# Planner durations, buffers for row sums, early weight loads and a folded softmax scale in an attention stage

## The chip, the cores and the metric

The kernel runs on one core of one Trainium2 chip. The metric is the device time of one execution in microseconds (us). Five engines take part: TensorE (PE, with its weight loads as PEld), VectorE (DVE), ScalarE (ACT), GpSimd (POOL) and SyncE (SP), which here only starts transfers. Each engine works through its own queue in the order of the program and meets the others at semaphores.

## The reference

The program is a decoder trunk of two layers over 1040 positions (16 learned ones ahead of 1024) and width 1024, in float32. Layer 0 mixes tokens with a recurrent scan and a pooling mixer; layer 1, which the change concerns, with differential attention of 8 heads, each with two sets (c = 0, 1) of 64-wide queries and keys and one set of 128-wide values:

```
def one_block(args):                       # a block of 128 queries
    qblk, start = args
    s = jnp.einsum('bqhcd,bkhcd->bhcqk', qblk, k).astype(jnp.float32) * scale   # scale = 64 ** -0.5 = 1/8
    qpos = start + jnp.arange(Q_BLOCK)
    mask = kpos[None, :] <= qpos[:, None]
    s = jnp.where(mask, s, -jnp.inf)
    p = jax.nn.softmax(s, axis=-1)
    attn = p[:, :, 0] - lam * p[:, :, 1]
    return jnp.einsum('bhqk,bkhe->bqhe', attn.astype(v.dtype), v)

o = rmsnorm(causal_diff_attention(q, k, v, lam), subln_w, SUBLN_EPS) * (1.0 - lam_init)
m = o.reshape(B, L, D_MODEL) @ w_out
h = h + rmsnorm(m, g[1])
f = sq_relu_mlp(rmsnorm(h, g[2]), mlp_w1[i], mlp_w2[i])
h = h + rmsnorm(f, g[3])
```

The 16 learned positions are dropped from the output; their queries are not computed in layer 1.

## The kernel before, in words

`Trunk.run` calls four stages: `mixer0`, `late(0)`, `mixer1`, `late(1)`. A mixer ends with its output projection begun, and `late` finishes the projection and does both norms and the MLP. Full float32 products are made of three passes of a rounded format: each operand is split into a high part (a cast on ScalarE, for instance `opb<-raw`) and a low part (a subtraction on VectorE or POOL), and `mm3` multiplies high by high, low by high and high by low.

The order of `mixer1` isn't the order of its code. A `Recorder` stands in for the five engines: `Recorder.call` notes each instruction with the tiles that it reads and writes and with a planned duration (`cost`), and `Flow.order` then lists them anew, each engine always taking, of what could start first, the task with the longest way to the end. The list is then issued as it stands (all these instructions carry line 298 in the profile, the replay in `call`), and each engine's queue has that order. So a planned duration changes no instruction, but the places of instructions on all engines. `late` has a `Flow` of its own, with its own durations (`F.act`, `F.dve`, `F.pe`), which are not touched.

`mixer1`, per head: `attn_in` projects queries, keys and values of the next head in three stretches of columns (`rows`, `vals`; PSUM tiles of the two-buffer ring `dps`), turns queries and keys by position (`ab`), regroups them through transfers (`qkd<-ab`, in `heads`) and splits them (`halves`: `qst` for the queries, `kh` and `kl` for the keys, the latter on VectorE and POOL). `turn` transposes and splits the values (tiles that are called `spare` too). `attn_block` does the softmax of one block of 128 queries for both c, over 144, 272, ... 1040 keys: score matmuls into `s` (ring `sps`, two buffers of 1024 columns; the last 16 of 1040 in a tile `tr` of the one-buffer ring `tps`), row maxima in `m` (the tile `m2`), exponentials on ScalarE into `vt` and `p` (the tiles p0 and p1; `vt` is the name of the buffer that p0 shares) with row sums to `m`, a reciprocal, and the difference of both. `attn` transposes the weights (`tr`), splits them (`ah`) and multiplies with the values (`av`, ring `aps`, one buffer). The head's output goes to DRAM (`o1d<-cau`) and is loaded back (`ho<-o1d`) as an operand `opa` of the output projection. `early` computes the first part of that projection beside head 7, and writes it with `part<-pz`.

Row sums for the input norm: `settle` multiplies a stretch of accumulated squares (`rsa`) by ones on TensorE into a tile of `psum()`, which is the ring `dps`, and takes the reciprocal root. `mixer1` calls it for stretches 1 and 2.

In `late(1)` the rest of the projection needs five raw weight tiles: two of `in_wl` (640 columns used), then three of `in_wo`. Each is loaded (line 677), cast (678) and subtracted (679) into the operands `opb`; the stored first part returns with `ac<-part` (681), and line 699 multiplies into `bank`. For layer 0 the first two raw tiles are loaded in `mixer0`.

Of the kernel before, what the change touches and what calls it, by code (L numbers as in the profile page):

```python
# [7 lines left out]
F32 = mybir.dt.float32  # L8
F32R = mybir.dt.float32r
AF = mybir.ActivationFunctionType  # L10
ALU = mybir.AluOpType
# [3 lines left out]
P = 128  # L15
T = 1040
NM = 16
# [46 lines left out]
LW = ((768, 768, 1024, 1024), (640, 640, 1024, 1024, 1024))  # L64
# [138 lines left out]
class Recorder:  # L203
# [60 lines left out]
    def call(self, eng, op, args, kw):  # L264
        aps = [x for x in list(args) + list(kw.values()) if hasattr(x, "tensor") and hasattr(x, "ap")]
        out = kw.get("out", args[0] if args else None)
        w = [out] + ([kw["accum_out"]] if kw.get("accum_out") is not None else [])
        r = [x for x in aps if not any(x is y for y in w)]
        n = max(math.prod(int(k) for k in x.shape[1:]) for x in aps)
        psum = any(x.space == PSUM for x in aps)  # L270
        size = 0
        if op.startswith("dma"):
            cost = {"POOL": 1.0, "SP": .47}.get(eng, .38)
            words = math.prod(int(k) for k in out.shape)
            run = min(self.run_of(x) for x in aps)
            size = words / run * (8 + .0367 * 4 * run) / 16e3 * 350e3
        elif eng == "PE":
            cols, x = math.prod(int(k) for k in args[0].shape[1:]), args[1]
            if op == "transpose":
                cost = .115  # L280
            elif x.dtype == F32R:
                cost = max(cols / 2400 + .014, .108)
            elif x.dtype == F32:
                cost = 2 * max(2 * cols / 2400 + .003, .111)
            else:
                cost = max(cols / 2400 + .01, .06)
        elif eng == "DVE":
            column = any(x.shape[-1] == 1 for x in aps)
            cost = n / (480 if op == "tensor_tensor_scan" else 960) + .07 + (.06 if column else 0.0) + (.08 if psum and out.shape[0] < P else 0.0)
        elif eng == "ACT":  # L290
            wide = max(len(x.shape) for x in aps) > 2
            cost = n / (1200 if wide or not psum else 1700) + (.165 if wide and psum else .2 if wide else .1)
            cost += sum(.09 for k in ("scale", "bias") if hasattr(kw.get(k), "ap"))
        else:
            cost = n / 450 + .15
        fn = getattr(getattr(self.real, {"PE": "tensor", "DVE": "vector", "ACT": "scalar", "POOL": "gpsimd", "SP": "sync"}[eng]), op)
        port = eng == "POOL" or eng == "DVE" and not psum and len(aps) > 2
        one = eng, cost, lambda: fn(*args, **kw), r, w  # L298
        if self.held is not None:
            self.held.append(one)  # L300
        else:
            self.keep(eng, cost, [one[2]], r, w, port and not size, size)
# [27 lines left out]
class Trunk:  # L330
# [156 lines left out]
    def rows(self, d, t0, W):  # L487
        return d.rearrange("(k p) t -> p k t", p=P)[:, :, t0:t0 + W]

    def settle(self, t0, W):  # L490
        acc = self.rsa[:, t0:t0 + W]
        ps = self.psum()[:, :W]
        self.nc.tensor.matmul(ps, self.con[:, K_ONE:K_ONE + P], acc, start=True, stop=True)
        self.rsqrt(ps, 1024, 1e-6, acc, self.tmp("rp", 3)[:, :W])

# [66 lines left out]
    def late(self, l, xs, part, hin, hmid, hout, pre, rsb):  # L562

        nc, tc, A = self.nc, self.tc, self.A
# [32 lines left out]
        S = [rp.tile([P, NH], F32, name=f"ss{i}") for i in (0, 1)]  # L597
# [71 lines left out]
        n = self.lw_n  # L669
        rl = [[("L", i, 0), ("L", i, 1)] + [c for b, a in self.lw_at[i] for c in nX(("B", b), 0, 4 * NH)] for i in range(len(n))]  # L670
        for i in range(len(n)):
            hi, lo = self.lw(i)
            if True:
                z = ("R", i % 4 // 2, i % 2)
                raw = R[i % 4 // 2][:, i % 2, :n[i]]
                if l or i > 1:
                    F.dma(lambda raw=raw, i=i: nc.sync.dma_start(raw, self.lw_src(l, i)), n[i] * 512, w=[z])
                F.act(n[i], lambda raw=raw, hi=hi: nc.scalar.copy(hi, raw), r=[z], w=[("L", i, 0)])  # L678
                F.dve(n[i], lambda raw=raw, hi=hi, lo=lo: tt(lo, raw, hi.bitcast(F32), op=ALU.subtract), r=[z, ("L", i, 0)], w=[("L", i, 1)])
            if i < 2:  # L680
                F.dma(lambda h=i: nc.sync.dma_start(m[h][:, :ne], self.rows(part, off + NH * h, NH)), ne * P * 4 * NH, w=sum((nM(i, k) for k in range(ne)), []))
# [209 lines left out]
        n, hs = H  # L891
# [753 lines left out]
    def mixer1(self, hn):  # L1645
# [4 lines left out]
        with tc.tile_pool(name="dps", bufs=2, space=PSUM, reuse_waits="tile") as dps, \  # L1650
# [47 lines left out]
            for h in range(8):  # L1698
# [5 lines left out]
                i = 0  # L1704
# [10 lines left out]
            for c in range(4):  # L1715
                xs[c].append(self.x7[c])
            self.late_x = xs
            rec.flow.run()
        self.nc = tc.nc
        return part  # L1720

    def attn_in(self, h, hn):
# [7 lines left out]
        def rows(nme, c):  # L1730
            q = nme == "q"
            t0, W = CH[c]
            if c == 0:
                if h:
                    w[nme] = self.weights(self.A["w_qkv"][(0 if q else 8) + h])
                tl[nme] = ep.tile([P, T], F32, tag="ab", name=self.nm("ab"), bufs=2)
            off = NM if (q and c == 0) else 0
            if h == 0 and c < 2:
                ps = self.first[nme][:, c * 512:c * 512 + 512]
            else:  # L1740
                ps = self.dps.tile([P, 512], F32, tag="d", name=self.nm("psq"))
                project(nme, c, ps, off)
            if h == 0 and nme == "k":
                if c > 0:
                    self.settle(t0, W)
                for j in (0, 1):
                    z = cs[:, j, t0:t0 + W]
                    nc.vector.tensor_tensor(z, z, self.rsa[:, t0:t0 + W], op=ALU.mult)
            s = slice(t0 + off, t0 + W)
            ab = tl[nme]  # L1750
            b = ep.tile([P, CW], F32, tag="rp", name=self.nm("rp"), bufs=3)
            nc.vector.tensor_tensor(b[0:64, off:W], ps[64:128, off:W], cs[64:128, 1, s], op=ALU.mult)
            nc.vector.tensor_tensor(b[64:128, off:W], ps[0:64, off:W], cs[0:64, 1, s], op=ALU.mult)
            nc.vector.tensor_tensor(ab[:, s], ps[:, off:W], cs[:, 0, s], op=ALU.mult)
            nc.gpsimd.tensor_tensor(ab[:, s], ab[:, s], b[:, off:W], op=ALU.add)
# [15 lines left out]
        def halves(nme):  # L1771
            for c in (0, 1):
                d = tl[nme, c]
                if nme == "q":
                    st = ep.tile([P, 1024], F32R, tag="qst", name=self.nm("qst"), bufs=2)
                    nc.scalar.copy(st, d[:, :1024])
                    nc.vector.tensor_tensor(st[64:128], d[64:128, :1024], st[64:128].bitcast(F32), op=ALU.subtract)
                    res["q", c] = st
                else:
                    kh = ep.tile([P, T], F32R, tag="kh", name=self.nm("kh"), bufs=2)  # L1780
                    kl = ep.tile([P, T], F32R, tag="kl", name=self.nm("kl"), bufs=2)
                    nc.scalar.copy(kh, d)
                    for a, b, e in ((0, 640, nc.vector), (640, T, nc.gpsimd)):
                        e.tensor_tensor(kl[:, a:b], d[:, a:b], kh[:, a:b].bitcast(F32), op=ALU.subtract)
                    res["k", c] = (kh, kl)
# [36 lines left out]
    def attn_block(self, h, i, qkv):  # L1822
# [7 lines left out]
        for c in (0, 1):  # L1830
# [18 lines left out]
                        nc.tensor.matmul(out(x0, x1), self.identb, self.maskb[:, x0 - m0:x1 - m0], start=False, stop=True)  # L1849
            S.append(sp)  # L1850
            if L > 512:
                nc.vector.tensor_reduce(m2[:, c:c + 1], sp[:, :L0], axis=mybir.AxisListType.X, op=ALU.max)
        if L <= 512:
            s3 = S[0].rearrange("p (c k) -> p c k", c=2)[:, :, :L]
            nc.vector.tensor_reduce(m2[:, 0:2], s3, axis=mybir.AxisListType.X, op=ALU.max)
        if se is not None:
            nc.vector.tensor_reduce(m2[:, 4:6], se[:, :2 * NM].rearrange("p (c k) -> p c k", c=2),
                                    axis=mybir.AxisListType.X, op=ALU.max)
            nc.vector.tensor_tensor(m2[:, 0:2], m2[:, 0:2], m2[:, 4:6], op=ALU.max)
        nc.vector.tensor_scalar(m2[:, 0:2], m2[:, 0:2], -0.125, None, op0=ALU.mult)  # L1860
        pr = []
        for c in (0, 1):
            p = ep.tile([P, T], F32, tag=f"p{c}", name=self.nm("p"), bufs=1 if c else 3)
            nc.scalar.activation(p[:, :L0], S[c][:, :L0], AF.Exp, bias=m2[:, c:c + 1], scale=0.125, accum_out=m2[:, 2 + c:3 + c])
            if se is not None:
                nc.scalar.activation(p[:, 1024:T], se[:, c * NM:(c + 1) * NM], AF.Exp, bias=m2[:, c:c + 1], scale=0.125,
                                     accum_out=m2[:, 6 + c:7 + c])
            pr.append(p)
        if se is not None:
# [238 lines left out]
```

## Time and profile before

| what | value |
|---|---|
| median of 3 runs | 2774.11 us (2773.92 to 2783.99) |
| profiled execution, its time | 2776.32 us |
| its span in the trace | 2774.5 us |
| its mean granted TensorE clock | 0.973 |
| attention stage in the trace, with the handover | about 1410 to 2037.5 us |
| of it a steady head | 66.0 us |

The profile is of one execution. A row of the timeline has its start and its length (of all instructions in the row where x2 or more stands at its end), the engine, the line, the operation, what it writes and reads, and, in brackets, how long the engine was idle before and which engine's work ended that. In the tables of stretches `PEclk` is the TensorE clock that was granted, as a share of full speed.

### The profile page before, as it was taken

The page shows a single profiled execution, that of the slowest core. Times are in us where ns is not written, and L with a number is a line of the kernel's source. Part 1 is how long each engine was busy: PE and PEld are TensorE (multiplying, and loading weights), DVE is VectorE, ACT ScalarE, POOL GpSimd, SP SyncE. Part 2 cuts the span into 40 slices and gives each one's busy share as a digit, 9 for nine tenths or more (in the row PEclk, how much of TensorE's full clock was granted, in tenths as well). Part 3 has the DMA queues.
Part 4 walks back from the last instruction along what each step waited for, and adds up shares of the span by engine and source line. Part 5 has one row for each costly group of instructions (what it writes and reads, how often), then busy time and mean ns, then how long its engine had stood idle before and what let it go on. Part 6 is the DMA issues. An engine that isn't in the chain of part 4 may idle for free.

```text
span 2774.5 us, 44830 instructions
## 1 busy us (share of the span) xinstructions
PE 2613.0 (94%) x16950; PEld 2378.8 (86%) x16950; DVE 2021.7 (73%) x3742; ACT 1344.0 (48%) x2779; POOL 289.9 (10%) x410
## 2 busy tenths in 40 slices
PE   7999998899999999999969999998989999999997
PEld 6899897899899999999967888887887788778877
DVE  5356867534977777888787777777538778778888
ACT  6456766544633334343345555555636333443343
POOL 0111334220000000000023222222000000000000
PEclk9999999899999999999989999998999999999998
DMA  4456777554324345443332222222143243543443
GB/s 155 168 184 190 239 218 221 179 161 151 143 102 169 137 163 194 168 154 135 109 120 74 65 69 62 62 60 83 55 147 144 106 167 136 193 187 137 152 159 122
DMA packets 198576, 391.28 MB, mean 141 GB/s; under 512 B 59984, under 2 KB 122328, under 8 KB 185944
## 3 DMA queue, kind: packets, MB, share of 16 engines
q1 hardware_dynamic: 171176, 348.24, 37.7%
q10 hardware_dynamic: 27184, 40.18, 4.0%
q8 instruction: 133, 2.18, 0.3%
q14 instruction: 83, 0.68, 0.1%
HBM read 240.06 MB, written 131.38 MB: 134 GB/s over the span
## 4 chain that ended last, share of the span: by engine, by line
PE 60%; DVE 11%; ACT 5%; issue 2%; DMA 2%; POOL 0%; SPq 0%; DVEq 0%; ACTq 0%; POOLq 0%
PE bank L699 43%; PE ps L298 9%; PE s L298 2%; PE av L298 2%; ACT vt L298 1%; PE tr L298 1%; DVE m L298 1%; PE xs L298 1%; ACT p L298 1%; DVE opb L826 1%; DVE ac L1080 1%; DMA hh<-hid 1%; DVE ac L1081 1%; DVE vt L298 1%; DVE ac L1009 1%
## 5 line engine op out<-in xcount | busy, mean ns | idle before, releaser
L699 PE MATMUL bank<-opa,wp 128*128 128x260 f32 (+1 forms) x3296 | 657.5, 319 | 8.3 <-DVE wp L790 4.9
L699 PEld LDWEIGHTS bank<-opa,wp 128*128 128x128 f32 x3296 | 516.9, 188 | 59.7 <-DVE wp L790 6.4
L298 PE MATMUL ps<-opa,wp 128*128 128x346 f32 (+3 forms) x1600 | 345.5, 326 | 7.9 <-DVE spare L298 2.7
L699 PE MATMUL bank<-opb,wp 128*128 128x260 f32 (+1 forms) x1150 | 347.5, 323 | 1.8 <-DVE ac L1009 1.8
L298 PEld LDWEIGHTS ps<-opa,wp 128*128 128x128 f32 x1600 | 260.7, 191 | 20.0 <-issue 4.7
L298 PE MATMUL ps<-opa,whi 128*128 128x346 f32 (+2 forms) x1008 | 269.1, 329 | 4.9 <-DVE ys L298 4.2
L699 PE MATMUL bank<-opa,hh 128*128 128x260 f32 (+1 forms) x1112 | 241.1, 321 | 7.9 <-DVE hh L790 5.3
L699 PEld LDWEIGHTS bank<-opb,wp 128*128 128x128 f32 x1150 | 216.2, 188 | 20.9 <-issue 2.2
L1009 DVE TENSOR_TENSOR ac<-bank,ac 128x520 f32<-128x520 f32 (+1 forms) x256 | 171.5, 691 | 67.5 <-PE bank L699 66.1
L699 PE MATMUL bank<-opa,opb 128*128 128x260 f32 (+4 forms) x1168 | 207.1, 307 | 13.4 <-ACT opb L678 10.1
L699 PEld LDWEIGHTS bank<-opa,hh 128*128 128x128 f32 x1112 | 185.8, 191 | 24.4 <-DVE hh L790 5.8
L699 PEld LDWEIGHTS bank<-opa,opb 128*128 128x128 f32 x1168 | 169.2, 195 | 24.3 <-ACT opb L678 10.5
L298 PEld LDWEIGHTS ps<-opa,whi 128*128 128x128 f32 x1008 | 181.7, 193 | 6.8 <-DVE ys L298 5.0
L699 PE MATMUL bank<-opb,hh 128*128 128x260 f32 (+1 forms) x616 | 180.4, 326 | 0.0
L789 ACT CAST wp<-raw 128x512 fp32r<-128x512 f32 (+1 forms) x138 | 80.4, 584 | 185.2 <-PE bank L699 181.2
L298 PE MATMUL ps<-opa,wlo 128*128 128x346 f32 (+2 forms) x504 | 158.6, 315 | 0.0
L789 ACT CAST wp<-ss 128x512 fp32r<-128x512 f32 (+1 forms) x130 | 76.7, 590 | 164.3 <-PE bank L699 143.5
L699 PE MATMUL bank<-opa,tt 128*128 128x260 f32 (+1 forms) x648 | 130.4, 318 | 0.2 <-DVE tt L790 0.2
L699 PEld LDWEIGHTS bank<-opb,hh 128*128 128x128 f32 x616 | 117.6, 191 | 10.0
L298 POOL TENSOR_TENSOR wpx<-raw,wp 128x1024 fp32r<-128x1024 f32 (+1 forms) x14 | 35.2, 2516 | 817.2 <-PE bank L699 742.5
L699 PE MATMUL bank<-opb,opb 128*128 128x256 f32 (+4 forms) x456 | 111.3, 307 | 0.5 <-DVE tt L755 0.5
L699 PEld LDWEIGHTS bank<-opa,tt 128*128 128x128 f32 x648 | 102.1, 188 | 9.5 <-DVE tt L790 0.4
(372 smaller groups left out, 5820.5 us busy)
## 6 DMA issues: line engine op xcount, KB each, us to landing
raw<-in_w_dram SPq DMA_DIRECT2D x64, 1024.0 KB
hid<-ac SPq DMA_DIRECT2D x14, 1820.0 KB
hid<-ac SPq DMA_DIRECT2D x14, 1792.0 KB
hh<-hid SPq DMA_DIRECT2D x23, 1040.0 KB
hh<-hid SPq DMA_DIRECT2D x23, 1024.0 KB
pk<-sg ACTq DMA_DIRECT2D x32, 704.0 KB
lt<-pk SPq DMA_DIRECT2D x32, 704.0 KB
raw<-in_w_qkv_dram SPq DMA_DIRECT2D x24, 512.0 KB
```

Source lines behind the costliest of these rows:

```text
L298: one = eng, cost, lambda: fn(*args, **kw), r, w
L699: nc.tensor.matmul(ps, use(x), use(y), start=start and i == j == 0, stop=i == len(ws) - 1 and j == 2, skip_group_check=not start)
L789: F.act(n, lambda: nc.scalar.copy(use(t[0][:, :n]), src), r=rd, w=[z[0]] + claim)
L826: F.dve(4 * NH, lambda: tt(lo, use(src), hi.bitcast(F32), op=ALU.subtract), r=rd + wh, w=wl)
L1009: F.dve(NH, lambda d=d, q=q: tt(sv(d), q, sv(d), op=ALU.add), r=nq + nd, w=nd, ps=True)
L1080: F.dve(W, lambda d=d, k=k: stt(d, d, self.gcol(l, 3, k), y, op0=ALU.mult, op1=ALU.mult), r=nd + [ny], w=nd)
L1081: F.dve(W, lambda d=d, k=k: tt(d, d, use(H3[k // 4][:, k % 4, :W]), op=ALU.add), r=nd + [("H", k // 4, k % 4)], w=nd)
```

## The change

Five edits, all in or around `mixer1`:

1. Planned durations in `Recorder.call`: a starting float32r matmul of 400 columns or more counts 0.085 us more; ScalarE's work on PSUM of 400 columns or more counts n/1200 + 0.06 in place of n/1700 + 0.1; an accumulated row sum (`accum_out`) 0.1 more.
2. `settle` takes its PSUM tile from the ring `tps` (stretch 1) and `aps` (stretch 2) in place of `dps`.
3. The loads of the two raw `in_wl` tiles of layer 1 are recorded at the end of `mixer1`, not in the flow of `late(1)`.
4. The queries are scaled by 1/8 where they are split: the cast becomes an `activation` with a scale, the subtraction a `scalar_tensor_tensor`. The exponentials lose their scale.
5. The row maxima are written negated (`negate=True`), the two parts of the longest block are joined with `min`, and the multiplication of `m` by -1/8 goes.

```diff
             elif x.dtype == F32R:
-                cost = max(cols / 2400 + .014, .108)
+                cost = max(cols / 2400 + .014, .108) + (.085 if cols >= 400 and kw.get("start") else 0.0)
...
             cost = n / (1200 if wide or not psum else 1700) + (.165 if wide and psum else .2 if wide else .1)
+            if psum and n >= 400:
+                cost = n / 1200 + .06
+            if kw.get("accum_out") is not None:
+                cost += .1
...
-    def settle(self, t0, W):
+    def settle(self, t0, W, pool, tag):
         acc = self.rsa[:, t0:t0 + W]
-        ps = self.psum()[:, :W]
+        ps = pool.tile([P, 512], F32, tag=tag, name=self.nm("ps"))[:, :W]
...
-                if l or i > 1:
+                if i > 1:
                     F.dma(lambda raw=raw, i=i: nc.sync.dma_start(raw, self.lw_src(l, i)), n[i] * 512, w=[z])
...
             self.late_x = xs
+            self.lw_n = LW[1]
+            for i in (0, 1):
+                nc.sync.dma_start(self.R[0][:, i, :self.lw_n[i]], self.lw_src(1, i))
             rec.flow.run()
...
-                    self.settle(t0, W)
+                    self.settle(t0, W, *((self.tps, "tr"), (self.aps, "av"))[c - 1])
...
-                    nc.scalar.copy(st, d[:, :1024])
-                    nc.vector.tensor_tensor(st[64:128], d[64:128, :1024], st[64:128].bitcast(F32), op=ALU.subtract)
+                    nc.scalar.activation(st, d[:, :1024], AF.Copy, scale=0.125)
+                    nc.vector.scalar_tensor_tensor(st[64:128], d[64:128, :1024], 0.125, st[64:128].bitcast(F32), op0=ALU.mult, op1=ALU.subtract)
...
-                nc.vector.tensor_reduce(m2[:, c:c + 1], sp[:, :L0], axis=mybir.AxisListType.X, op=ALU.max)
+                nc.vector.tensor_reduce(m2[:, c:c + 1], sp[:, :L0], axis=mybir.AxisListType.X, op=ALU.max, negate=True)
...
-            nc.vector.tensor_tensor(m2[:, 0:2], m2[:, 0:2], m2[:, 4:6], op=ALU.max)
-        nc.vector.tensor_scalar(m2[:, 0:2], m2[:, 0:2], -0.125, None, op0=ALU.mult)
+            nc.vector.tensor_tensor(m2[:, 0:2], m2[:, 0:2], m2[:, 4:6], op=ALU.min)
...
-            nc.scalar.activation(p[:, :L0], S[c][:, :L0], AF.Exp, bias=m2[:, c:c + 1], scale=0.125, accum_out=m2[:, 2 + c:3 + c])
+            nc.scalar.activation(p[:, :L0], S[c][:, :L0], AF.Exp, bias=m2[:, c:c + 1], accum_out=m2[:, 2 + c:3 + c])
```

The lines of the kernel after stand four lower (298 is 302 there), and a tile in a shared buffer goes by the name of the first that used it: the ring of `tr` begins with a `ps`, that of `av` with another `ps`, and the ring `dps` is called `psv`.

TensorE at the start of `mixer1`, where the products of the first values begin. Before, the row sum of stretch 1 stands there alone:

```order
L298 MATMUL s_1_13729<-opa_75,wp_6334 128x346
L298 MATMUL ps_0_13735<-rsa,con 128x346
L298 MATMUL ps_1_13736<-opa_70,spare_0_13737 128x348
L298 MATMUL ps_1_13736<-opa_70,spare_0_13739 128x348
L298 MATMUL ps_1_13736<-opa_70,spare_0_13737 128x348 x2
```

The one of stretch 2 stands some fifty rows on, among the products of a projection:

```order
L298 MATMUL ps_1_13736<-opa_76,wp_6333 128x346
L298 MATMUL ps_1_13736<-opa_76,wp_6332 128x346
L298 MATMUL ps_0_13735<-rsa,con 128x346
L298 MATMUL ps_1_13736<-opa_76,wp_6332 128x346
L298 MATMUL ps_1_13736<-opa_76,wp_6333 128x346
```

Now both are together, each with a buffer of its own, and the second no longer parts the projection:

```order
L302 MATMUL s_1_13729<-opa_75,wp_6334 128x346
L302 MATMUL ps_0_13735<-rsa,con 128x346
L302 MATMUL ps_0_13745<-rsa,con 128x346
L302 MATMUL psv_0_13743<-opa_70,spare_0_13736 128x348
L302 MATMUL psv_0_13743<-opa_70,spare_0_13738 128x348
```

VectorE in head 7, the block of 656 keys (`m_0` its maxima and sums, `s_0` and `s_1` its scores, `cau` the normalizing of an earlier output, `m_3` the block before). Before:

```order
L298 TENSOR_REDUCE m_0_13752<-s_0_13728 128x1
L298 SCALAR_TENSOR_TENSOR cau_13720<-ps_1_13736,cau_13720 128x512
L298 TENSOR_TENSOR ah_3_13761<-tr_0_13757,ah_2_13760 128x512
L298 TENSOR_REDUCE m_0_13752<-s_1_13729 128x1
L298 SCALAR_TENSOR_TENSOR cau_13723<-cau_13720,cau_13723 128x512
L298 TENSOR_TENSOR opa_71<-ho_0_13765,opa_71 128x256
L298 TENSOR_TENSOR ah_1_13759<-tr_0_13757,ah_0_13758 128x512
L298 TENSOR_SCALAR m_0_13752<-m_0_13752 128x2
```

Now, with the first reduction ahead of the rest of the block before, and nothing between the second one and the exponentials:

```order
L302 TENSOR_REDUCE m_0_13754<-s_0_13728 128x1
L302 RECIPROCAL m_3_13757<-m_3_13757 128x2
L302 TENSOR_TENSOR axh_1_13764<-ps_0_13735,axh_0_13763 16x128
L302 TENSOR_SCALAR m_3_13757<-m_3_13757,nlam 128x1
L302 TENSOR_REDUCE m_0_13754<-s_1_13729 128x1
L302 SCALAR_TENSOR_TENSOR vt_0_13740<-p_0_13758,m_3_13757,vt_0_13740 128x528
```

The reductions moved up past the `cau`, `ah` and `opa` rows, and the multiplication is gone.

SyncE at the handover from `mixer1` to `late(1)`. Before, the second `in_wl` tile stands behind `ac<-part`, which waits for the stored first part:

```order
L298 DMA raw_743<-in_wo_dram 128x768
L677 DMA raw_743<-in_wl_dram 128x640
L677 DMA raw<-in_wo_dram 128x1024 x2
L681 DMA ac_19218<-part_13700 128x5x512
L677 DMA raw_743<-in_wl_dram 128x640
L763 DMA hh_19216<-h_68 128x4x512
```

Now both stand ahead of it:

```order
L302 DMA raw_743<-in_wo_dram 128x768
L302 DMA raw_743<-in_wl_dram 128x640 x2
L681 DMA raw<-in_wo_dram 128x1024 x2
L685 DMA ac_19156<-part_13700 128x5x512
L767 DMA hh_19154<-h_68 128x4x512
```

The second weight tile moved up past two loads of `in_wo` and the wait of `ac<-part`.

More of the change, by code (lines that the diff above doesn't have):

```diff
@@ L1851, in attn_block @@
             if L > 512:
-                nc.vector.tensor_reduce(m2[:, c:c + 1], sp[:, :L0], axis=mybir.AxisListType.X, op=ALU.max)
+                nc.vector.tensor_reduce(m2[:, c:c + 1], sp[:, :L0], axis=mybir.AxisListType.X, op=ALU.max, negate=True)
         if L <= 512:
             s3 = S[0].rearrange("p (c k) -> p c k", c=2)[:, :, :L]
-            nc.vector.tensor_reduce(m2[:, 0:2], s3, axis=mybir.AxisListType.X, op=ALU.max)
+            nc.vector.tensor_reduce(m2[:, 0:2], s3, axis=mybir.AxisListType.X, op=ALU.max, negate=True)
         if se is not None:
             nc.vector.tensor_reduce(m2[:, 4:6], se[:, :2 * NM].rearrange("p (c k) -> p c k", c=2),
-                                    axis=mybir.AxisListType.X, op=ALU.max)
-            nc.vector.tensor_tensor(m2[:, 0:2], m2[:, 0:2], m2[:, 4:6], op=ALU.max)
-        nc.vector.tensor_scalar(m2[:, 0:2], m2[:, 0:2], -0.125, None, op0=ALU.mult)
+                                    axis=mybir.AxisListType.X, op=ALU.max, negate=True)
+            nc.vector.tensor_tensor(m2[:, 0:2], m2[:, 0:2], m2[:, 4:6], op=ALU.min)
         pr = []
@@ L1863, in attn_block @@
             p = ep.tile([P, T], F32, tag=f"p{c}", name=self.nm("p"), bufs=1 if c else 3)
-            nc.scalar.activation(p[:, :L0], S[c][:, :L0], AF.Exp, bias=m2[:, c:c + 1], scale=0.125, accum_out=m2[:, 2 + c:3 + c])
+            nc.scalar.activation(p[:, :L0], S[c][:, :L0], AF.Exp, bias=m2[:, c:c + 1], accum_out=m2[:, 2 + c:3 + c])
             if se is not None:
-                nc.scalar.activation(p[:, 1024:T], se[:, c * NM:(c + 1) * NM], AF.Exp, bias=m2[:, c:c + 1], scale=0.125,
+                nc.scalar.activation(p[:, 1024:T], se[:, c * NM:(c + 1) * NM], AF.Exp, bias=m2[:, c:c + 1],
                                      accum_out=m2[:, 6 + c:7 + c])
```

## The prediction

> **What bounds the kernel now.** I read the engines' shares first, then a table of stretches of the attention stage (the only stage whose instructions move), then TensorE's waits in those stretches, and last single rows.
>
> ```profile
> PE 2613.0 (94%) x16950; PEld 2378.8 (86%) x16950; DVE 2021.7 (73%) x3742; ACT 1344.0 (48%) x2779; POOL 289.9 (10%) x410
> ```
>
> TensorE is busy for 94% of the span, so only its idle time, or work done at a low clock, can be won. Four stretches of the stage (start-up, one steady head, head 7, the handover to the output projection); the numbers are length, then busy time of each engine with its instructions, the granted clock and the transfers:
>
> ```profile
> core 0: us, PE busy (x) PEld busy (x) DVE busy (x) ACT busy (x) POOL busy (x), PEclk, DMA share, GB/s
> 1425.00:1478.00 53.00, 43.64 (x241) 39.50 (x242) 35.45 (x70) 17.51 (x34) 19.40 (x15) 0.87 0.26 71
> 1589.39:1655.45 66.06, 64.26 (x424) 58.09 (x423) 50.70 (x100) 38.28 (x77) 16.75 (x16) 1.00 0.24 65
> 1920.00:1980.00 60.00, 47.80 (x276) 39.15 (x275) 45.44 (x94) 39.39 (x90) 3.25 (x4) 0.80 0.25 71
> 2028.40:2037.50 9.10, 0.68 (x3) 0.33 (x2) 2.15 (x3) 3.28 (x5) 0.00 (x0) 0.75 1.03 388
> ```
>
> Read the first number against the second. A steady head wastes 66.06 - 64.26 = 1.8 us, so six of them hold 10.8 us at most. Head 7 wastes 60.00 - 47.80 = 12.2 us, and its clock of 0.80 costs about 47.80 x 0.20 = 9.6 us more: 21.8 us in all. The start wastes 9.4 us, the handover 8.4 us. VectorE is busy for 50.70 of 66.06 us in a steady head: shortening it gains nothing by itself there.
>
> What TensorE waits for, in a steady head (first fence) and in head 7 (second):
>
> ```profile
> PE s L298 <- ACT vt L298: 0.9, 1, 0.9
> ```
> ```profile
> PE tr L298 <- ACT p L298: 2.9, 1, 2.9
> PE s L298 <- ACT p L298: 2.4, 2, 1.8
> PE tr L298 <- DVE vt L298: 1.4, 1, 1.4
> ```
>
> Nearly all of it is the softmax chain: score matmuls `s`, maxima `m`, exponentials `vt`/`p`, release of the score buffer or transposes of the weights.
>
> **The change, part by part.**
>
> *Maxima with the sign turned.* 64 `TENSOR_SCALAR` on `m` go. The rows of one block of 656 columns, and of the last block of head 6:
>
> ```profile
> 1958.90 0.84 DVE L298 TENSOR_REDUCE m<-s 128x1 f32<-128x656 f32 x1 [1.09 <-PE s L298]
> 1960.85 0.83 DVE L298 TENSOR_REDUCE m<-s 128x1 f32<-128x656 f32 x1
> 1963.51 0.16 DVE L298 TENSOR_SCALAR m<-m 128x2 f32<-128x2 f32 x1
> 1963.70 0.81 ACT L298 ACTIVATE vt<-s,m 128x656 f32<-128x656 f32 x1 [0.53 <-DVE m L298]
> ```
> ```profile
> 1925.48 2.87 POOL L298 TENSOR_TENSOR kl<-qkd,kh 128x400 fp32r<-128x400 f32 x2 [9.36 <-ACT kh L298]
> 1926.41 0.70 DVE L298 TENSOR_TENSOR m<-m 128x2 f32<-128x2 f32 x1
> 1927.37 1.00 DVE L298 TENSOR_SCALAR m<-m 128x2 f32<-128x2 f32 x1
> 1928.41 1.11 ACT L298 ACTIVATE vt<-s,m 128x1024 f32<-128x1024 f32 x1 [1.17 <-DVE m L298]
> 1931.27 0.48 PE L298 MATMUL tr<-con,vt 128*128 128x128 f32 x1 [2.88 <-ACT p L298]
> ```
>
> The removed instruction wrote both columns, so the first exponential waited for both reductions. Now, in the blocks of 528 to 912 columns, the first waits for its own alone: the chain is shorter by one 0.16 and one reduction (0.83 here). On VectorE that is 64 x 0.16 = 10.2 us, worth nothing directly, since it is not full. On the chain, in the last block of head 6, the instruction took 1.00 beside POOL's `kl` and the exponential began 0.04 after it ended, with the 2.88 of TensorE hanging on it: I take 1.2 us there (1928.41 back to about 1927.2). Head 7's next blocks that show waits (528 and 656) get 0.8 each. `min` for `max` has the same operands and shape: nothing.
>
> *Queries scaled in their cast.* The rows that the two new forms are nearest to, the old cast and subtraction, and a scaled `ACTIVATE` and a `SCALAR_TENSOR_TENSOR` of like width:
>
> ```profile
> 1659.02 1.05 ACT L298 CAST qst<-qkd 128x1024 fp32r<-128x1024 f32 x1
> 1660.11 1.24 DVE L298 TENSOR_TENSOR qst<-qkd,qst 64x1024 fp32r<-64x1024 f32 x1 [0.26 <-ACT qst L298]
> 1654.87 1.18 ACT L298 ACTIVATE vt<-vt,m 128x1040 f32<-128x1040 f32 x1
> 1656.72 1.29 DVE L298 SCALAR_TENSOR_TENSOR vt<-p,m,vt 128x1040 f32<-128x1040 f32 x1
> ```
>
> At worst 0.13 + 0.05 per pair, 16 pairs: 2.9 us of engine time, beside TensorE's transposes; on the path only before a head's first scores, so 0 to +1.3 us (7 x 0.18). I take 0. The exponential loses an immediate only: no price.
>
> *The planner's durations.* They order every engine in the stage. The exponential of 1024 columns was planned as 1024/1700 + 0.1 + 0.09 = 0.79 us, now 1024/1200 + 0.06 + 0.1 + 0.09 = 1.10. Two such exponentials in line, and a starting score matmul with the one behind it:
>
> ```profile
> 1651.23 1.12 ACT L298 ACTIVATE vt<-s,m 128x1024 f32<-128x1024 f32 x1
> 1652.33 1.11 ACT L298 ACTIVATE p<-s,m 128x1024 f32<-128x1024 f32 x1
> 1643.88 0.48 PE L298 MATMUL s<-kh,qst 128*128 128x512 f32 x1
> 1644.20 0.39 PE L298 MATMUL s<-kl,qst 128*128 128x512 f32 x1
> ```
>
> From start to start (1651.23 to 1652.33) it is 1.10: the new figure is the true one. For the starting matmul it is 0.32 (1643.88 to 1644.20): old plan 0.227, new 0.312. So the new order rests on better numbers, and in the order of the program a head's first scores stand some 6 us of TensorE work (by the planned durations) earlier. In steady heads its worth lies between -1.8 (all waste gone) and, since the only wait there on the score buffer is 0.9, +1.0 per head if that wait doubles. With the shorter chain I take -0.5 for each of six: -3.0 (range -10.8 to +6). In head 7, beside the 1.2 + 2 x 0.8 above, I let the clock give back 1.7 of its 9.6: -4.5 in all (range -21.8 to +5, the latter the largest two waits, 2.9 and 2.4, once more).
>
> *Row sums in other PSUM buffers.* The start-up:
>
> ```profile
> 1425.04 1.49 PE L298 MATMUL ps<-rsa,con 128*128 128x346 f32 x2 [10.76 <-DVE rsa L691]
> 1432.11 9.30 PE L298 MATMUL ps<-opa,spare 128*128 128x348 f32 x47 [2.10 <-POOL spare L298]
> 1442.68 0.74 PE L298 MATMUL ps<-rsa,con 128*128 128x346 f32 x2
> 1455.08 1.08 PE L298 MATMUL ps<-con,vt 128*128 128x128 f32 x7 [1.27 <-DVE ab L298]
> 1458.24 0.43 PE L298 MATMUL ps<-opa,wp 128*128 128x348 f32 x1 [2.08 <-DVE spare L298]
> ```
>
> The second row sum moves from 1442.68 to directly behind the first, under the wait for POOL that ends at 1432.11, and the third projection of the queries goes ahead of the values. The 10.76 stays: its operand is not earlier. ScalarE, which has the three steps of the reciprocal root to do, has nothing else then. Of the later waits the 1.27 should go, its operand coming earlier, and a third of the 2.08: -2.0, between -5.5 (2.10 + 1.27 + 2.08) and +2.1 (the POOL wait once more).
>
> *Raw weights early.* Both `raw<-in_wl` now stand ahead of `raw<-in_wo` and of the waiting `ac<-part` in SP's queue. The handover:
>
> ```profile
> 2028.55 0.83 ACTq L298 DMA_DIRECT2D part<-pz  x2
> 2030.18 0.83 DVE L679 TENSOR_TENSOR opb<-raw,opb 128x640 fp32r<-128x640 f32 x1 [12.37 <-ACT opb L678]
> 2034.90 2.16 ACT L678 CAST opb<-raw 128x1024 fp32r<-128x1024 f32 x2 [4.75 <-DMA part<-pz]
> 2036.00 0.58 PE L699 MATMUL bank<-opa,opb 128*128 128x256 f32 x1 [7.54 <-ACT opb L678]
> 2037.46 0.80 PE L699 MATMUL bank<-opa,opb 128*128 128x256 f32 x2 [0.88 <-DVE opb L679]
> ```
>
> Before, the first products needed casts that wait for `part<-pz` to land at 2034.90, then VectorE. After, the products of the first early weight need only the cast and the subtraction that end at 2031.0 (2030.18 + 0.83), while the second one's low part overwrites a buffer that a `part<-pz` still reads: that landing stays late, and 0.83 behind it TensorE flows, at about 2035.6 instead of 2037.46. I take -1.9, between 0 (the third weight is then awaited instead) and -3.5 (the first early products also shorten what follows). Behind it TensorE waits for the `wo` casts as before.
>
> Sum: -2.0 - 3.0 - 4.5 - 1.9 = -11.4 us against the profiled execution's 2776.3: 2764.9. The runs' median, 2774.1, lies 2.2 lower, so I say 2764, which is 0.4% below the median. About 0.5% (13.9 us) is what a measurement of this kernel tells from no change.
>
> **The rivals.**
>
> *Head 7 collapses (2755).* Its stretch holds 21.8 us. Ten of its sixty microseconds:
>
> ```profile
> 1930.00:1935.00 5.00, 2.24 (x6) 1.26 (x6) 2.68 (x7) 2.98 (x10) 0.00 (x0) 0.50 0.87 198
> 1935.00:1940.00 5.00, 3.65 (x18) 3.53 (x19) 3.54 (x4) 3.66 (x6) 0.19 (x1) 0.50 0.29 80
> ```
>
> If the shorter chain keeps TensorE busy enough that the clock stays near 1.00, half of the 12.2 and 6 of the 9.6 go: -12, and with -5 in the heads 2776.3 - 2 - 5 - 12 - 1.9 = 2755. For it: the three largest waits above all hang on the chain. Against: the transfers of the last queries (DMA share 0.87 in the first slice) do not shorten. The Trainium skill ("TensorE: Matmul & The Clock Gate", Part 1: The HAM clock gate) says that the clock halves after an idle window of about 3.4 us and comes back after as long a busy one. The 10.76 of idleness with 0.87 behind it agrees; in head 7 the trace differs, since the clock was already at 0.50 after a longest gap of 2.88. By the page, read strictly, gaps below its window cost no clock, and all of the 9.6 would be back, 2752 in place of 2755; I give that reading 0.05 of the 0.25 below.
>
> *Hidden anyway (2772).* The heads are full of TensorE work (97%), and an earlier score may just move the wait. Then only start-up and handover count: 2776.3 - 3.9 = 2772.
>
> *Slower (2790).* TensorE takes its queue in order; a score matmul placed before the exponentials have released its buffer holds everything behind it. The scores stand earlier now, so that wait (0.9 in a steady head) could grow. It decides once it is over 2.6 us longer in each of six heads, with nothing gained elsewhere (6 x 2.6 = 15.6, and 2776.3 - 3.9 + 15.6 = 2788.0, 0.5% above the median). At 3.0 each the time is 2790. For it: the new plan still leaves out 0.2 us of each chain's hops, and all heads share one order. Against: its durations are nearer to the rows than the old ones, and the chain has become shorter.
>
> **How the numbers follow.** Forecast 0.50, collapse 0.25, hidden 0.17, slower 0.08. The forecast's own range is 2757 to 2770; about 0.07 of its chance lies under 2760.2 (0.5% below the median). Faster: 0.25 - 0.02 (the collapse's upper end) + 0.07 = 0.30; slower 0.07, the part of its case above 2788.0; the rest, 0.63, is within 0.5%. The range 2750 to 2779 leaves out some 0.06 below (a full collapse) and 0.09 above.
>
> **What would show it.** Right, if in the profile after: the first exponential of a block of over 512 columns starts behind the first reduction; both `rsa` matmuls stand together ahead of 1432; head 7's stretch is shorter by 4 to 5 us with its clock above 0.80; TensorE's wait before the first output product falls from 7.54 to about 2, with another of 4 to 5 for the second weight's low part. Wrong, if steady heads leave 64.3 of 66 us (their waits on `s` grow or vanish), or if head 7's stretch falls under 50 us.

## The result, and the profile after

The changed kernel took 2762.31 us (median of 6 runs, 2751.65 to 2765.51) against 2775.6 for the kernel before: a ratio of 0.9929, 95% interval 0.9908 to 0.9951. Measured once more it was 2757.27 against 2773.83, 0.9937 (0.992 to 0.9954). The forecast, 2764, held as a total. Its terms did not: the attention stage became 24.1 us shorter, not 11.4, and the profiled execution gave 8.5 us of that back ahead of the stage and 2.2 behind it.

The page after (engines, then the granted clock) differs little from that of before, since the work is the same but for 64 small instructions of VectorE:

```profile
PE 2614.4 (95%) x16950; PEld 2381.0 (86%) x16950; DVE 2015.0 (73%) x3678; ACT 1341.0 (49%) x2779; POOL 292.9 (11%) x410
PEclk9999999899999999999989999999999999999999
```

To set the two traces side by side I cut the stage at the same instructions in each: first row sum on TensorE, first scores, the start of the scaling of p0 in each head's last block (eight of them), and the last point at which TensorE waits before the output products flow. The first cuts and the last two scalings after:

```profile
1433.49 1.49 PE L302 MATMUL ps<-rsa,con 128*128 128x346 f32 x2 [10.97 <-DVE rsa L695]
1473.50 0.33 PE L302 MATMUL s<-kh,qst 128*128 128x144 f32 x1 [0.40 <-DVE qst L302]
1928.36 1.16 ACT L302 ACTIVATE vt<-vt,m 128x1040 f32<-128x1040 f32 x1 [0.49 <-DVE m L302]
1981.94 1.16 ACT L302 ACTIVATE vt<-vt,m 128x1040 f32<-128x1040 f32 x1 [0.23 <-DVE m L302]
```

| part of the stage, us | before | again | after | again | forecast of the change |
|---|---|---|---|---|---|
| start-up: row sum to first scores | 43.3 | 43.5 | 40.0 | 40.1 | -2.0 |
| first scores to head 0's scaling | 53.1 | 53.1 | 48.0 | 48.0 | not in the sum |
| head 0 to head 6, six heads | 410.3 | 410.4 | 406.9 | 407.1 | -3.0 |
| head 6 to head 7 | 61.7 | 61.7 | 53.6 | 53.3 | -4.5 |
| head 7 to the flow of output products | 44.1 | 43.5 | 39.8 | 41.8 | -1.9 |
| whole stage | 612.4 | 612.2 | 588.3 | 590.2 | -11.4 |
| start of the stage in the trace | 1425.0 | 1427.2 | 1433.5 | 1430.0 | 0 |

The stretches after, in the form of the prediction's table (start-up, a steady head, head 6 to 7):

```profile
1433.49:1473.50 40.01, 34.53 (x191) 31.53 (x191) 28.11 (x54) 13.44 (x23) 17.71 (x14) 0.87 0.35 94
1654.14:1720.02 65.88, 64.83 (x423) 58.03 (x422) 51.01 (x91) 37.67 (x76) 17.80 (x15) 1.00 0.24 66
1928.36:1981.94 53.58, 47.60 (x325) 41.33 (x326) 40.89 (x83) 39.73 (x95) 2.44 (x3) 0.91 0.25 77
```

and the last of them as it was before, cut at the same instructions:

```profile
1931.71:1993.39 61.68, 53.82 (x336) 45.72 (x336) 42.36 (x91) 40.32 (x93) 2.22 (x3) 0.84 0.24 69
```

That stretch lost 1.9 us of idleness (7.9 to 6.0) and 6.2 us of busy time. By an estimate from the two rows (busy time times clock: 45.2 before, 43.3 after) some 4 of the 6.2 us are a clock that stands at 0.91 instead of 0.84. The steady head lost nothing: its wait on the score buffer went from 0.9 to 0.2, and TensorE filled the room with the same work (64.83 busy in place of 64.26 of about 66 us).

Why 24.1 us in the stage are 13.5 in the span (2774.5 to 2761.0): 8.5 were lost ahead of it. The two stages that run first have the same instructions in the same order in both kernels. In the second one the first matmul that sums over its rows (before, then after) stands 9.2 us later already, so the time was lost in the very first stage:

```profile
679.77 1.04 PE L739 MATMUL bank<-ss,con 128*128 128x260 f32 x4
```
```profile
688.94 1.04 PE L743 MATMUL bank<-ss,con 128*128 128x260 f32 x4
```

### The profile page after: what moved, and what is told of

Its sections match the earlier page's. It is cut to its first block, busy times and chain, and to the rows that moved or that the text cites. A ratio compares the mean times of both kernels' runs of the same rounds, so it can differ in the third digit from the quotient of the medians.

```text
span 2761.0 us, 44772 instructions
## 1 busy us (share of the span) xinstructions
PE 2614.4 (95%) x16950; PEld 2381.0 (86%) x16950; DVE 2015.0 (73%) x3678; ACT 1341.0 (49%) x2779; POOL 292.9 (11%) x410
## 4 chain that ended last, share of the span: by engine, by line
PE 63%; DVE 10%; ACT 3%; issue 2%; DMA 2%; POOL 0%; SPq 0%; DVEq 0%; ACTq 0%; POOLq 0%
PE bank L703 44%; PE psv L302 9%; PE ps L302 5%; PE s L302 3%; DVE m L302 1%; PE xs L302 1%; DVE ac L1084 1%; DVE ac L1085 1%; DVE opb L830 1%; DVE ac L1013 1%; DVE ac L780 1%; DVE rp L302 1%; DMA hh<-hid 0%; PE ob L302 0%; DVE opa L1120 0%
## 5 line engine op out<-in xcount | busy, mean ns | idle before, releaser
L302 PE MATMUL psv<-opa,wp 128*128 128x346 f32 (+3 forms) x1600 | 343.9, 323 | 2.1 <-ACT pz L302 0.7
L302 PEld LDWEIGHTS psv<-opa,wp 128*128 128x128 f32 x1600 | 259.3, 190 | 11.8 <-DVE ab L302 3.2
```

## The experiments

The four independent edits were first put on the kernel before, one at a time. "Stage" is counted as above.

**The planner's durations alone.**

```diff
+ (.085 if cols >= 400 and kw.get("start") else 0.0)      # starting float32r matmul
+ if psum and n >= 400: cost = n / 1200 + .06              # ScalarE
+ if kw.get("accum_out") is not None: cost += .1
```

> Only the planner's new durations, on the kernel before. The stage is counted in the trace from the first row sum of the attention stage to TensorE's steady flow of output products: 612.4 us before, 588.3 after. Theory A (the order makes the gain): 612 falls to about 594 to 598, with head 6 to 7 (61.7 us between the last scalings of p0 before, 53.6 after) at 54 to 56. Theory B (the shorter softmax chain makes it): the stage stays at 606 to 614 and that stretch at 59 or more. Time: A about 2758 to 2763, B 2770 or more.

Measured: 2786.8 us, 1.0034 (1.0018 to 1.0049), slower. Stage 621.5: start-up 48.1, steady heads 69.1, head 6 to 7 54.8. Both theories missed the stage and the time; head 6 to 7 is as A had it. So the new order does shorten head 7, but costs 3.0 us in each steady head. Of these, 1.4 are idleness of TensorE (1.8 to 3.2), the rest longer busy time of the same matmuls at the same clock. TensorE's longest waits in a steady head of it:

```profile
PE tr L302 <- DVE vt L302: 1.6, 1, 1.6
PE s L302 <- ACT vt L302: 0.8, 1, 0.8
```

**Scaled queries and negated maxima alone.**

```diff
- nc.scalar.copy(st, d[:, :1024])
+ nc.scalar.activation(st, d[:, :1024], AF.Copy, scale=0.125)
- nc.vector.tensor_scalar(m2[:, 0:2], m2[:, 0:2], -0.125, None, op0=ALU.mult)
  ...                  # and negate=True, min, no scale in the exponentials
```

> Only the scaled queries and the negated maxima, so without the multiplication of m that joined both columns. Theory A: stage 607 to 613 us, head 6 to 7 above 59. Theory B: stage 596 to 602, head 6 to 7 at 53 to 56. The old plan still orders the instructions. Time: A 2769 to 2775, B about 2760.

Measured: 2760.48, 0.9935 (0.9914 to 0.9955). Stage 594.4, head 6 to 7 52.8: theory B, a little beyond its figures. Three quarters of the stage's gain come from these two edits alone, under the old order. In the time of whole runs they can't be told from all five (0.9929 and 0.9937).

**Row sums in other buffers alone** (`settle` on `tps` and `aps`).

> Only the row sums in other PSUM buffers. Both theories: from the first row sum to the first scores 43.3 us before becomes 40 to 42 (after: 40.0); the heads keep their 66.0; head 6 to 7 stays at 61 to 62. Time 2770 to 2774. If head 0, which went from 53.1 us (first scores to its last scaling) to 48.0 in the changed kernel, gains here, it was the start-up's backlog; if not, the order.

Measured: 2768.84, 0.9968 (0.9954 to 0.9981). Start-up 41.5, head 0 48.8 (53.1 before), the heads 66.0, head 6 to 7 61.5; stage 604.5. So the start-up's gain has a second half that lies behind the first scores, which the prediction did not look at.

**Early weight loads alone** (both `raw<-in_wl` recorded in `mixer1`).

> Only the early loads of the two raw weight tiles. From the last block's scaling to the flow of output products: 44.1 us before, 39.8 after. Both theories: 40 to 42 here, of which 4.0 are the handover itself (last pz copy to flow 9.3 before, 5.4 after); time 2770 to 2772. If the handover stays at 9.3, the order of the last transfers made it.

Measured: 2774.44, 0.9995 (0.9981 to 1.0009). Stage 606.7; last scaling to flow 41.8, of which last `pz` copy to flow 7.0 (9.3 before). The 41.8 is the expected size, the 2.3 of the handover itself is not the expected 4.0, and in the time of whole runs neither is seen. Head 6 to 7 was 58.9 here with an unchanged order, 2.8 shorter than before.

Next, what in the scaled queries and negated maxima gained, and whether the planner's part is needed.

**All but the planner's durations.**

> The changed kernel with the planner's old durations. The new durations alone made the stage longer (612.4 to 621.5 us), the three other edits alone shorter (by 18.1, 8.0 and 5.7). Theory C (the new durations cost their 9 us here too): stage 578 to 583, time about 2745 to 2751, the fastest of all. Theory D (with the shorter chain the new order no longer hurts, and it brings what the others lack): stage 588 to 593, time 2759 to 2765, no faster than the changed kernel.

Measured: 2758.16, 0.9937 (0.9917 to 0.9956), stage 588.4: theory D. The new durations cost 9.0 us in the stage alone and nothing beside the other edits.

**Same scaling, both columns still multiplied together; then column by column** (on the kernel before):

```diff
- nc.vector.tensor_scalar(m2[:, 0:2], m2[:, 0:2], -0.125, None, op0=ALU.mult)
+ nc.vector.tensor_scalar(m2[:, 0:2], m2[:, 0:2], -1.0, None, op0=ALU.mult)              # joint
+ for c in (0, 1): nc.vector.tensor_scalar(m2[:, c:c + 1], m2[:, c:c + 1], -1.0, ...)    # split
```

> On the kernel before: queries scaled in their cast, exponentials without scale, maxima not negated, and the multiplication of both columns of m kept (now by -1). Theory E (what gained was that the first exponential no longer waits for both reductions): stage 609 to 614 us, head 6 to 7 at 60 to 62, as before. Theory F (the scale taken out of the exponential, or the new cast, gained): stage 594 to 600.

> The same, but the multiplication by -1 done column by column, in two instructions of 0.15 us or so: as many maxima and one instruction more on VectorE, and the first exponential waits for its own reduction alone. Theory E: most of the gain of the negated maxima (stage 612.4 to 594.4) comes back, stage 594 to 601, in spite of 64 instructions more than g_joint. Theory G (the gain is VectorE's 64 instructions less, or their place in its queue): 609 to 616.

Measured: joint 2780.08, 1.0024 (1.0006 to 1.0042), stage 610.7, head 6 to 7 58.9; split 2768.34, 0.9975 (0.9957 to 0.9993), stage 604.2, head 6 to 7 55.8. The joint kernel rules theory F out: the scale is worth nothing. The 1.7 us less in its stage are no gain either: in two stretches TensorE's instructions stand in the order of the kernel before, yet of these the start-up took 45.6 us at a clock of 0.78 (43.3 at 0.84), and head 6 to 7 58.9 at 0.89 (61.7 at 0.84). So 2 to 3 us in either stretch say nothing of an edit.

The split kernel falls between: 6.5 us come back with 64 instructions more (3.5 in head 0, 3.1 from head 6 to 7), and 9.8 more (604.2 to 594.4) with the instruction gone. Of the 9.8, 2.3 lie in the start-up (45.5 at a clock of 0.78, 43.2 at 0.84), which holds no softmax. So theory E is right for roughly half, G for the rest. The split also changes a second thing: none of its 128 multiplications on 128x1 numbers took over 0.16 us, even while GpSimd worked, whereas six of the joint kernel's 64 on 128x2 took 0.4 to 1.2. None of the six lies from head 6 to 7, but two lie in head 0, and there no run parts the freed column from this.

**The changed kernel with a multiplication of both columns by 1.0 put back.**

> The changed kernel with a multiplication of both columns of m by 1.0 put back in front of the exponentials, so that both wait for both reductions again. Theory E: the stage goes from 588.3 to 600 or more, with head 6 to 7 above 56 and steady heads at 68 to 70, as with the new durations alone. Theory G: at most 590 to 594 (64 x 0.16 us, part of it hidden).

Measured: 2776.5, 0.9999 (0.9986 to 1.0012): the whole gain in time is gone. Stage 608.6, steady heads 69.1, as with the durations alone: theory E's figures, but head 6 to 7 stayed at 54.8, under the 56 that theory E named. The last block of a steady head shows what the small instruction costs. In this kernel (GpSimd's two `kl`, then its `ab`, as rows of their own):

```profile
1652.22 2.65 POOL L302 TENSOR_TENSOR kl<-qkd,kh 128x400 fp32r<-128x400 f32 x2
1654.82 0.80 POOL L302 TENSOR_TENSOR ab<-ab,rp 128x346 f32<-128x346 f32 x1
```
```profile
1653.87 1.00 DVE L302 TENSOR_TENSOR m<-m 128x2 f32<-128x2 f32 x1
1654.91 0.73 DVE L302 TENSOR_SCALAR m<-m 128x2 f32<-128x2 f32 x1
1655.74 1.12 ACT L302 ACTIVATE vt<-s,m 128x1024 f32<-128x1024 f32 x1 [2.97 <-DVE m L302]
...
1661.59 0.44 PE L302 MATMUL ps<-con,vt 128*128 128x128 f32 x2 [1.64 <-DVE vt L302]
```

and in the changed kernel:

```profile
1649.49 0.80 POOL L302 TENSOR_TENSOR ab<-ab,rp 128x346 f32<-128x346 f32 x1 [0.17 <-DVE ab L302]
```
```profile
1649.57 0.73 DVE L302 TENSOR_TENSOR m<-m 128x2 f32<-128x2 f32 x1
1650.85 1.11 ACT L302 ACTIVATE vt<-s,m 128x1024 f32<-128x1024 f32 x1
```

Read the ends: the join of the maxima ends at 1654.87, just as the `kl` pair does; the multiplication at 1655.64, 0.02 after `ab`; after the change the join ends at 1650.30, 0.01 after its `ab`. Two instructions on 128x2 numbers, 0.16 each elsewhere, wait out GpSimd's. The Trainium skill ("SBUF — State Buffer", section "SBUF: two separate sides") states that GpSimd and a VectorE instruction with two SBUF inputs, or in a two-port mode, share a pair of ports as an exclusive lock, held for a whole instruction. The rows of the join, which has two inputs, agree; those of the multiplication, which has one, show the same wait, and no run shows its mode. Summed over the stage (busy us, mean ns), the 64 multiplications cost, before and with the new durations alone:

```profile
L298 DVE TENSOR_SCALAR m<-m 128x2 f32<-128x2 f32 x64 | 13.9, 223 | 0.9
```
```profile
L302 DVE TENSOR_SCALAR m<-m 128x2 f32<-128x2 f32 x64 | 22.5, 353 | 0.6
```

So the new order sets them beside GpSimd's work, on the path to the exponential, and the other edit takes them away. In each steady head of the kernel with the durations alone, and of the one with the multiplication put back, three `m<-m` are long, 1.72, 1.00 and 0.73 us. At 0.16 each they would take 2.97 us less, and these heads are 3.0 us longer than before, where the steady heads from 1588 to 1787 have none above 0.2. This is agreement in size; a wait of TensorE behind them is shown for the last block alone. The one of 1.72, in the middle of a head of the durations alone, beside GpSimd's `wp`:

```profile
1694.80 2.40 POOL L302 TENSOR_TENSOR wp<-raw,wp 128x1024 fp32r<-128x1024 f32 x1 [6.46 <-ACT wp L302]
1695.51 1.72 DVE L302 TENSOR_SCALAR m<-m 128x2 f32<-128x2 f32 x1
1697.26 0.81 ACT L302 ACTIVATE vt<-s,m 128x656 f32<-128x656 f32 x1 [2.54 <-DVE m L302]
```

The planner has a notion of this wait: `Recorder.call` marks (`port`) all GpSimd work, and VectorE's with more than two operands outside PSUM, as excluding each other. The multiplication of `m` has two operands, so it is not marked, and the plan sees no price in setting it there.

The freed first column is seen in a block of 912 keys, before and after (the row of x2 holds two reductions of 1.1 us):

```profile
1633.42 1.10 DVE L298 TENSOR_REDUCE m<-s 128x1 f32<-128x912 f32 x1
1638.13 1.11 DVE L298 TENSOR_REDUCE m<-s 128x1 f32<-128x912 f32 x1 [0.53 <-PE s L298]
1639.28 0.17 DVE L298 TENSOR_SCALAR m<-m 128x2 f32<-128x2 f32 x1
1639.58 1.03 ACT L298 ACTIVATE vt<-s,m 128x912 f32<-128x912 f32 x1
```
```profile
1636.30 2.11 DVE L302 TENSOR_REDUCE m<-s 128x1 f32<-128x912 f32 x2
1637.43 1.02 ACT L302 ACTIVATE vt<-s,m 128x912 f32<-128x912 f32 x1 [1.89 <-DVE m L302]
1638.91 1.04 ACT L302 ACTIVATE p<-s,m 128x912 f32<-128x912 f32 x1
```

Before, the first exponential starts after both reductions; after, while the second one still runs.

**The two kernels again, and halves of the planner's edit** (on the changed kernel).

> The changed kernel once more, unaltered. In its first profile the attention stage was 24.1 us shorter than before but began 8.4 us later, behind two stages whose instructions stand in the same order in both kernels. Theory H (that start varies from execution to execution): the stage is 588 to 589 us again, its first row sum lies anywhere from 1422 to 1434. Theory I (the changed program itself makes what runs ahead of it slower): the first row sum is at 1432 to 1434 again and no execution is under 2756.

> The kernel before once more, unaltered: stage 612 to 613 us. Theory H: its first row sum anywhere from 1422 to 1434. Theory I: at 1424 to 1426 again.

> The changed kernel without the 0.085 for a starting matmul, so with the new durations of ScalarE alone. All new durations together left the stage at 588.3 against 588.4 without them; they gained 2.5 us at the handover and lost that in head 6. If ScalarE's durations make the handover's order: end 39 to 40 us, stage 586 to 590; if the matmul's do: end 42, stage 588 to 592.

> The changed kernel with the matmul's 0.085 and ScalarE's old durations: the other half. If ScalarE's durations make the handover's order: end 42, stage 588 to 592; if the matmul's do: end 39 to 40.

Measured: the changed kernel 2757.27, 0.9937; its stage began at 1430.0, that of the kernel before at 1427.2 (2777.8 in one run). ScalarE's durations alone: 2757.29, 0.9933 (0.9908 to 0.9958), stage 588.7, end 41.2. The matmul's alone: 2758.94, 0.9944 (0.9923 to 0.9966), stage 591.3, end 41.0. Neither half makes the handover's order: the changed kernel itself had 39.8 once and 41.8 once. No version is clear of the others.

## Why the prediction was right, and where it was not

*The total* came out within 2 us, in part by luck: the stage's terms were too small by half, and a start of the stage that was some 3 to 8 us later, forecast as no change, hid that. Over the twelve traces of the experiments the stage began between 1422.7 and 1434.0 with one and the same order ahead of it, and the two kernels' own pairs differ by 2.2 and 3.5, so a part is variation between executions (theory H); executions of the changed kernel as short as 2751.65, and its second start, outside 1432 to 1434, speak against theory I. But the kernels that hold three or more edits began at 1427.5 to 1434.0 and no single edit but one after 1427.4. Why stays open. The sum itself was not followed to the end: 11.4 off the median of 2774.1 is 2762.7, and 2764 was said.

*The planner's order* was the step that failed. "The new order rests on better numbers" was true of the rows and wrong as a reason for a gain: alone it lost 9.0 us, with the rest it was worth 0.1. The rival "slower" named that price (3.0 us in each head and 2790; the durations alone gave 3.0 and 2786.8), but as a wait on a score buffer, and that wait did not grow (0.9 before, 0.8). What grew is the wait of weight transposes on `vt` (0.4 to 1.6), behind the small instructions on `m`.

*Negated maxima.* The mechanism was right, the size not: 1.2 + 2 x 0.8 in head 7 and 0.5 per head, where the edit, with the scaled queries, brought 18.1 in the stage. It was priced at 0.16 us apart from one block, although that block's row of 1.00 beside GpSimd was quoted; and head 0 was left out of the sum: 53.1 to 47.6 with these edits alone. The join of the maxima, priced at nothing, takes 0.73 in place of 0.16 in the last block of a steady head of the changed kernel.

*Steady heads.* Six heads gained 3.4 for a forecast of 3.0, but at the ends (1.5 from head 0 to 1, 0.9 from 4 to 5, 1.5 from 5 to 6), not 0.5 in each: the three middle ones went from 66.0 to 66.2 on average. With the maxima alone TensorE is busy for 65.15 of 65.92 us, and the head is no shorter. So the 1.8 us were not waste to be had. Busy time in the profile is modelled, and the same 423 or 424 matmuls at a clock of 1.00 show 64.3 to 65.8 us of it, so length less busy time does not measure what can be won. What bounds such a head is not shown. The prediction's own sign of being wrong, heads that leave 64.3 of 66 as their waits on `s` vanish, came true here in part (64.83, 0.9 to 0.2).

*Head 7.* 8.1 for 4.5, and not the 4 to 5 that was to show it. Of the 8.1, 2.8 also came with an unchanged order (early loads alone, joint kernel). The rival "collapse" was right on the place: the waits on `p` are gone from the stretch. Before, cut at the same instructions, then after:

```profile
PE tr L298 <- ACT p L298: 2.9, 1, 2.9
PE s L298 <- ACT p L298: 2.6, 3, 1.8
```
```profile
PE ps L302 <- DVE vt L302: 3.7, 2, 2.7
PE s L302 <- DVE qst L302: 1.3, 1, 1.3
```

*Start-up.* -3.3 for -2.0. Both row sums stand together, but the second now waits 2.62 us for its operand at 1437.59, and still costs nothing: the wait lies under the one for GpSimd, as supposed.

*Handover.* The mechanism was right. After:

```profile
2016.41 0.72 ACT L302 COPY pz<-psv 128x256 f32<-128x256 f32 x2 [3.93 <-PE psv L302]
2018.44 0.39 PE L703 MATMUL bank<-opa,opb 128*128 128x256 f32 x1 [1.72 <-ACT opb L682]
2020.83 1.04 ACT L682 CAST opb<-raw 128x1024 fp32r<-128x1024 f32 x1 [1.81 <-DMA part<-pz]
2021.76 20.48 PE L703 MATMUL bank<-opa,opb 128*128 128x256 f32 x151 [1.84 <-DVE opb L683]
```

TensorE's wait before the first product is 1.72 us, forecast about 2. The second one, forecast at 4 to 5, is 1.84 and in the second trace 3.82. The flow starts 5.4 us behind the last copy, 7.3 in the second trace, 9.3 and 8.7 before. The 2.0 between the two traces of one kernel is the landing of `part<-pz`, 4.0 and 6.0 us after its issue (6.4 and 5.8 before). Counted from that landing, where the cast starts, the flow begins 2.6 and 2.5 us later before, 0.9 in both traces after: 1.6 gained, 1.9 forecast.

*Scaled queries and the missing scale* cost and gained nothing, as forecast: joint kernel 610.7 against 612.4.

## What to carry to other kernels

Price a tiny instruction by where it stands: on the chain that feeds the bounding engine, and beside GpSimd's work, 0.16 us became 0.7 to 1.7 here, and one that joins two columns makes the first wait for the second. A scheduler's truer durations are no gain by themselves; the order that they give must be run with each other edit, since the same durations lost 9 us without the shorter chain and nothing with it. And check a total that comes out right against its terms, cut at the same instructions in both traces.

## What the hardware showed that was not expected

Of VectorE's `m<-m` on 128x2 numbers in the stage, 8 of 80 took 0.3 us or more in the kernel before and 7 of 16 in the changed one, the others 0.14 to 0.17. Each of these 15 started while a GpSimd instruction ran and ended 0.01 to 0.03 us after it.

From 2 to 3 us of the start-up and of head 7 come and go with the granted clock. The joint kernel has the waits of before in head 7 (3.4, 2.6, 1.4 and 1.4 us, against 2.9, 2.6, 1.4 and 1.4), yet takes 58.9 us at a clock of 0.89, and the kernel before 61.7 at 0.84.

The clock fell without a long gap. In the kernel before, it went from 1.00 to 0.50 between 1916.5 and 1917, after gaps of at most 1.34 us since 1890:

```profile
1915.83 0.66 PE L298 MATMUL ps<-con,ab 128*128 128x128 f32 x4 [1.34 <-DVE ab L298]
```
```profile
1917.00:1920.00 3.00, 3.00 (x12) 2.38 (x12) 1.39 (x4) 2.86 (x7) 0.00 (x0) 0.50 0.54 173
```

It was at 0.50 again by 1927.5, ahead of the gap of 2.88, which lay between 1928.4 and 1931.27. So the prediction's "after a longest gap of 2.88" is a misreading; its point, that here the clock halved without a long gap, holds all the more.
